# A decoder block's seven-product matrix multiplications: one product's halves set between the others, and one left factor split by itself a panel ahead

## The chip, the cores and the metric

The program runs on one core of one Trainium2 chip. The metric is the device time of one execution in microseconds (us). TensorE (PE in the profile) multiplies and writes PSUM; VectorE (DVE) and ScalarE (ACT) read PSUM and work on SBUF; GpSimd (POOL) takes part in a few elementwise steps and issues the DMAs that add to what is already in SBUF; SyncE (SP) issues the plain loads and stores. Each engine works through its own instructions in order and waits for the others by semaphores.

## What is computed

One layer of a decoder trunk on 512 tokens of width 1024, in float32: a norm and one wide projection; a retention branch and a dilated attention branch, each gated; an output projection; an MLP with a squared relu; a gated embedding. The parts that matter here:

```python
z  = rmsnorm(x, g_mix) @ w_in
y  = retention_chunkwise(rq, rk, rv)             # then group norm
ret_branch = (silu(rg) * y) @ w_ret_out
x  = x + (gate_r * ret_branch + gate_a * att_branch) @ w_o
u  = rmsnorm(x, g_mlp) @ w_up
x  = x + square(relu(u)) @ w_down
x  = x + sigmoid(rmsnorm(x, g_ple) @ w_ple_gate) * (p @ w_ple_proj)
```

## The kernel before

**Three products for one.** Every float32 product is made of three matmuls in a faster type. `split_unit` (L233 to L254) makes `whi` (ACT, L247, a rounding copy) and `wlo` (DVE, L248, the rest) out of a raw weight tile; `mm3` (L256 to L261) multiplies stationary high by moving high, stationary high by moving low, and stationary low by moving high. Activations are kept as such pairs too (`hh` and `hl`, `uh` and `ul`).

**Weights come by a plan.** `make_plan` lists all weight tiles (512 KB each, "units") in the order of use. `fetch` loads them into raw tiles (`wraw`, 6 buffers); `units(n)` hands out the next n and lets `ahead` split AHEAD more in advance (2 or 3) into `wsp` (4 buffers of `whi`, 4 of `wlo`). So a unit's split waits until the unit four before it has been multiplied.

**Seven products.** Five of the larger multiplications (the output projection `w_o` and the four slices of `w_down`) and two in the retention (its value and gate columns) are done block by block with seven products in place of eight. `SEVEN` (L35) is their order: a pair is product and half (u = 0, 1; which half of the 512-long contraction), and None means both halves at once. In `seven_products` (L1079) an entry with a half uses one unit: two column blocks p of the left factor, 2 k each, 3 matmuls, which makes 12 matmuls of 128x128 by 128x512. `BANK` (L36) says which PSUM bank a product is summed in: products 1, 6, 7, 4 share bank "b", products 5 and 3 share bank "c", product 2 has bank "a". There is one of each for p = 0 and 1. Banks b and c are of the pool `psg` (4 banks), bank a is of `psa` (4 banks), from which transposes and all the attention's and retention's small matmuls take theirs. When a product's second half is done, `after` reads the bank: in `w_o` and `w_down` by one DVE instruction that adds it, scaled, to the running rows `x` (L1112); in the retention by ACT copies (m5, m1, m3), and DVE adds. A product that goes into a shared bank waits for the reader of the product before it in that bank.

**Right factors.** Some of the seven right factors are plain blocks of the weight (B11 for product 1, B21 for 2, B22 for 3), the others sums of blocks: T1 (product 5), T2 (6), T3 (7), T4 (4). T2 is made by a DMA that adds a block into T1's raw tile after T1 is split (`chained`, L225, on POOL's queue); T3 in the same way from B22's tile, T4 from T2's. In the retention T1 and T4 are made by a DVE add of raw tiles instead (`added`, L220 to L223).

**Left factors.** A left operand lies in a tile `z` as eight slices of 256 columns for each of four row blocks j; slice 0 is the plain block of product 1, slice 1 that of product 2, and slices 3 to 6 are sums (`LEFT`, L39). `seven_left` (L1067) makes the sums by three DVE instructions (L1071, L1073) and then rounds and splits all seven slices in one pair of instructions, 1792 columns wide: `uh` on ACT (L1076), `ul` on DVE (L1077). Each has four tiles (j = 0 to 3) of the pool `bigp` (16 buffers).

**Where z comes from.** In the MLP (`tail`, L1153 on), a pass f runs four `cols_gemm` panels: jj = 0, 1 and, for each, b = 0 and 1. A panel makes two row blocks (n = 0, 1). `act` evacuates each by relu and square on ACT: with b = 0 slice 0 and a side tile `a21`, with b = 1 slices 1 and 2, after which it calls `seven_left`. So block j = 3 is finished by the last panel, and `seven_gemm` begins right behind it on PE. In `mix` (L1007), the same is done for `w_o` by the gated branches: slice 0 by L1037 at branch "r" with kk < 4, and the rest at kk >= 4 (L1042, L1045). `mix` and the first three MLP passes are put in order by the scheduler when the program is built, PE always; ACT and DVE are held in program order in the `w_o` product and in the last MLP pass.

**Work between the products.** `tick` is called once for each (product, p) and, on even counts (each count in the tail), lets waiting work in: in the retention's second seven products that is `ret_head` of the first two heads (L953 to L992: scores `rs`, states `kv`, values `ry`, transposes `pt`, each in a bank of `psa`); in the `w_o` product and the last `w_down` product transposes of finished rows (`gain_T`), four matmuls each.

Of the kernel before, what the change touches and what calls it, by code (L numbers as in the profile page):

```python
# [13 lines left out]
AF = mybir.ActivationFunctionType  # L14
ALU = mybir.AluOpType
# [16 lines left out]
WARM = 7  # L32
GG = (2, 4)

SEVEN = ((1, 0), (5, 0), (1, 1), (5, 1), (3, 0), (3, 1), (6, 0), (6, 1), (2, 0), (2, 1), (7, None), (4, None))  # L35
BANK = {1: "b", 2: "a", 3: "c", 4: "b", 5: "c", 6: "b", 7: "b"}  # L36
FACTOR = {1: "B11", 2: "B21", 3: "B22", 4: "T4", 5: "T1", 6: "T2", 7: "T3"}
SEVEN_UNITS = [(FACTOR[m], v) for m, u in SEVEN for v in ((0, 1) if u is None else (u,))]
LEFT = {1: 0, 2: 1, 4: 2, 7: 3, 5: 4, 6: 5, 3: 6}  # L39
# [37 lines left out]
def R(ap):  # L77
    return ap.bitcast(F32R)


class Block:
# [87 lines left out]
    def plan_seven(self, w, r0, c1, c2, vector=False):  # L169

        cols = (c1, c2)
        q = lambda i, j, u: w[r0 + 512 * i + 256 * u : r0 + 512 * i + 256 * (u + 1), cols[j] : cols[j] + 512]
        n = len(self.plan)
        at = lambda name, u: n + SEVEN_UNITS.index((name, u))
        for name, u in SEVEN_UNITS:
            if name == "T1":
                src = q(0, 1, u) if vector else (q(0, 1, u), q(0, 0, u))
                if vector:
                    self.added[at("B11", u)] = at("T1", u)
            elif name == "T4" and vector:  # L180
                self.added[at("B21", u)] = at("T4", u)
                src = (None, at("T2", u))
            elif name[0] == "B":
                src = q(int(name[1]) - 1, int(name[2]) - 1, u)
            else:
                prev, ij = {"T2": ("T1", (1, 1)), "T3": ("B22", (0, 1)), "T4": ("T2", (1, 0))}[name]
                k = at(prev, u)
                self.chained[k] = q(*ij, u)
                src = (None, k)
            self.plan.append((src, None))  # L190
# [23 lines left out]
    def ahead(self, n):  # L214
        while len(self.loaded) < min(len(self.plan), self.used + n):
            i = len(self.loaded)
            self.fetch(i + 1)
            raw, g0 = self.raws[i]
            self.loaded.append(self.split_unit(raw, g0))
            if i in self.added:  # L220
                self.fetch(self.added[i] + 1)
                total = self.raws[self.added[i]][0]
                self.nc.vector.tensor_tensor(total, total, raw, op=ALU.add)  # L223
            if i in self.chained:
                self.nc.gpsimd.dma_start(raw, self.chained[i].rearrange("(k p) n -> p k n", p=P), accum_op=ALU.add)  # L225

# [780 lines left out]
    def mix(self, A, O):  # L1007
        nc = self.nc
        U, Z = [[None] * 4, [None] * 4], {}
        for pair in ((0, 2), (1, 3)):  # L1010
            parts = {}
            for br, act, nk, bo in (("a", O, H, 24), ("r", A, KD, 16)):
                if pair[0] and br == "r":
                    self.load_x()
                for cc in pair:
                    sg = []

                    def gate(n, ps):
                        s = self.tmp("gs")
                        b = bo + 2 * cc + n  # L1020
                        nc.vector.tensor_tensor(s, ps, self.r_free, op=ALU.mult)
                        nc.scalar.activation(s, s, AF.Sigmoid, bias=self.gcol[:, b : b + 1])
                        sg.append(s)

                    def branch(n, ps):
                        t = self.tmp("gt")
                        nc.vector.tensor_tensor(t, sg[n], ps, op=ALU.mult)
                        kk = 2 * cc + n
                        if br == "a":
                            parts[kk] = t  # L1030
                            return
                        j = kk % 4
                        if kk < 4:
                            m = self.tmp("gm")
                            nc.gpsimd.tensor_tensor(m, t, parts[kk], op=ALU.add)
                            z = self.big("z").rearrange("p a (b t) -> p (a b) t", b=2)
                            nc.scalar.activation(z[:, 0], m[:, :256], AF.Copy)  # L1037
                            Z[j] = z, m[:, 256:]
                        else:
                            z, a21 = Z.pop(j)  # L1040
                            v = lambda ap: ap.rearrange("p (h t) -> p h t", h=2)
                            nc.vector.tensor_tensor(z[:, 1:3], v(t), v(parts[kk]), op=ALU.add)  # L1042
                            for part, n in zip(U, ("uh", "ul")):
                                part[j] = self.big(n)
                            self.seven_left(z, a21, U, j)  # L1045

                    self.cols_gemm(self.hT, KD, gate)
                    for h in range(H):
                        if br == "a":
                            self.force(("O", h, NG - 1))  # L1050
                            self.force(("split", h))
                        else:
                            for i in range(NT):
                                self.force(("A", h, i))
                    self.cols_gemm(act, nk, branch)
        return U

# [8 lines left out]

    def seven_left(self, z, a21, U, j):  # L1067

        nc = self.nc
        both = a21.unsqueeze(1).to_broadcast([P, 2, 256])  # L1070
        nc.vector.tensor_tensor(z[:, 3:5], z[:, 0:3:2], both, op=ALU.subtract)  # L1071
        for o, x, y in ((5, 4, 0), (6, 1, 5)):
            nc.vector.scalar_tensor_tensor(z[:, o], z[:, x], -1.0, z[:, y], op0=ALU.mult, op1=ALU.subtract)  # L1073
        w = lambda t: t.rearrange("p a b -> p (a b)")[:, : 7 * 256]
        hi, lo, src = w(U[0][j]), w(U[1][j]), z[:, 0:7].rearrange("p a b -> p (a b)")
        nc.scalar.activation(R(hi), src, AF.Copy)  # L1076
        nc.vector.tensor_tensor(R(lo), src, hi, op=ALU.subtract)  # L1077

    def seven_products(self, left, after):  # L1079

        banks, begun = {}, set()
        for m, half in SEVEN:
            us = self.units(2 if half is None else 1)
# [35 lines left out]
    def tail(self, mx):  # L1119
        nc, a = self.nc, self.a  # L1120
# [31 lines left out]

        h3 = None  # L1153
        for f in range(NF // 2):
            U = [[self.big("uh") for _ in range(4)], [self.big("ul") for _ in range(4)]]
            Z = {}

            def act(b, j, ps):
                r = self.tmp("ur")
                nc.scalar.activation(r, ps, AF.Relu)  # L1160
                if b == 0:
                    z = self.big("z").rearrange("p a (b t) -> p (a b) t", b=2)
                    a21 = self.tmp("a21")[:, :256]
                    Z[j] = z, a21
                    nc.scalar.activation(z[:, 0], r[:, :256], AF.Square)
                    nc.scalar.activation(a21, r[:, 256:], AF.Square)
                else:
                    z, a21 = Z[j]
                    nc.scalar.activation(z[:, 1:3], r.rearrange("p (h t) -> p h t", h=2), AF.Square)
                    self.seven_left(z, a21, U, j)  # L1170

            for jj in range(2):
                for b in range(2):
                    self.cols_gemm(h2, KD, lambda n, ps: act(b, 2 * jj + n, ps))
            ready = None
            if f == NF // 2 - 1:
                h3 = self.new_act(2, "h3")
                halves = [0] * NT

                def ready(t, j):  # L1180
                    self.gain_T(xs[t], t, j, h3, "h3", 3)
                    halves[t] += 1
                    if halves[t] == 2:
                        self.mean_squares(xs[t], 3, lambda mean: factor(t, mean))

                def factor(t, mean):
                    v = self.small(1, "v")
                    mean(v)
                    nc.gpsimd.tensor_tensor(r3[:, t : t + 1], v, self.mhalf[:, :1], op=ALU.pow)
            if f == NF // 2 - 1:  # L1190
                order = self.tc.manual_schedule(engines={nc.scalar.engine, nc.vector.engine})
                order.__enter__()
                self.AHEAD = 3
            self.seven_gemm(U, xs, f2, ready)
# [84 lines left out]
```

## Time and profile before

| | |
|---|---|
| median of 3 runs | 990.71 us (990.6 to 991.1) |
| the profiled execution | 991.26 us, of which the span of instructions is 989.4 us |
| granted clock of TensorE | 0.999 |
| the `w_o` product | about 551 to 600 us of the span |
| the four `w_down` products | begin at about 648, 731, 814 and 897 us |
| the retention's two seven products | about 290 to 382 us |

The profile page gives busy time by engine, forty slices of the span, the chain of work that ended last, the groups of instructions and the DMA issues. In its rows "A <- B" after a group names who ended the idle time of the engine just before it. In a timeline a row is: start, duration, engine, line, operation, tile written <- tiles read, shapes, count. A matmul's duration (about 0.39 us) is longer than the distance between two of them (about 0.23 us), because they overlap in the array; PE therefore counts as busy through short stalls.

### The profile page before, as it was taken

What the parts mean: (1) busy time and instruction counts of PE and PEld (TensorE: products, weight loads), DVE (VectorE), ACT (ScalarE), POOL (GpSimd) and SP (SyncE); (2) the same over time, 40 slices, a digit from 0 to 9 for tenths busy, and PEclk for the clock granted to TensorE, in tenths of its full rate; (3) what the DMA queues carried; (4) which work ended last, traced back from release to release, by engine and by line L of the source; (5) the groups of instructions that cost most, each with busy time, mean ns of one, the idle gap of its engine ahead of it and who ended that gap; (6) DMA issues with size and microseconds to landing.
All of it is one profiled execution on the core that took longest, in us unless ns stands there. A gap on an engine that the chain in (4) does not pass through costs nothing.

```text
span 989.4 us, 12438 instructions
## 1 busy us (share of the span) xinstructions
PE 979.3 (99%) x4540; PEld 816.5 (83%) x4540; DVE 646.9 (65%) x1009; ACT 491.0 (50%) x999; POOL 111.2 (11%) x108
## 2 busy tenths in 40 slices
PE   9999999999999999999999999999999999999998
PEld 6888899889888878888888788878887887887886
DVE  7857665775969878454643885577557467656753
ACT  6635344446646556342332467554654564465551
POOL 0310120220001220101002200020011002002000
PEclk9999999999999999999999999999999999999999
DMA  9822122334257734233544666567558548556811
GB/s 327 269 85 87 44 85 86 103 125 127 86 123 199 195 102 128 66 93 98 185 111 110 134 185 208 136 121 214 141 111 195 151 120 169 166 140 111 260 66 53
DMA packets 88508, 136.49 MB, mean 138 GB/s; under 512 B 6096, under 2 KB 40576, under 8 KB 88448
## 3 DMA queue, kind: packets, MB, share of 16 engines
q1 hardware_dynamic: 75248, 110.52, 34.6%
q0 software_dynamic: 13056, 25.17, 15.4%
q8 instruction: 35, 0.57, 0.2%
q14 instruction: 25, 0.20, 0.1%
q10 hardware_dynamic: 144, 0.02, 0.0%
HBM read 131.46 MB, written 4.24 MB: 137 GB/s over the span
## 4 chain that ended last, share of the span: by engine, by line
PE 90%; DVE 4%; issue 3%; ACT 2%; DMA 1%; POOL 0%; SPq 0%; ACTq 0%; DVEq 0%
PE pg L259 26%; PE pg L260 26%; PE pg L261 26%; DVE wlo L248 2%; ACT uh L1076 2%; PE po L724 1%; PE ph L577 1%; PE pa L261 1%; PE pa L259 1%; PE pa L260 1%; PE pt L335 1%; PE sc L701 1%; DVE x L1112 1%; PE pe L669 1%; DMA raw<-in_w_in 1%
## 5 line engine op out<-in xcount | busy, mean ns | idle before, releaser
L248 DVE TENSOR_TENSOR wlo<-raw,whi 128x1024 fp32r<-128x1024 f32 (+1 forms) x178 | 210.2, 1191 | 97.5 <-ACT whi L247 96.1
L247 ACT ACTIVATE whi<-raw 128x1024 fp32r<-128x1024 f32 (+1 forms) x177 | 182.0, 1034 | 183.4 <-PE pg L261 99.5
L259 PE MATMUL pg<-whi,hh 128*128 128x512 f32 x344 | 138.0, 402 | 0.0
L261 PE MATMUL pg<-whi,hl 128*128 128x512 f32 x344 | 134.7, 392 | 0.0
L260 PE MATMUL pg<-wlo,hh 128*128 128x512 f32 x344 | 134.5, 391 | 0.0
L259 PE MATMUL pg<-h2h,whi 128*128 128x512 f32 x256 | 99.6, 389 | 0.0
L260 PE MATMUL pg<-h2l,whi 128*128 128x512 f32 x256 | 99.6, 389 | 0.0
L261 PE MATMUL pg<-h2h,wlo 128*128 128x512 f32 x256 | 99.6, 389 | 0.0
L259 PE MATMUL pg<-whi,uh 128*128 128x512 f32 x240 | 96.0, 401 | 2.4 <-ACT whi L247 0.7
L260 PE MATMUL pg<-wlo,uh 128*128 128x512 f32 x240 | 93.6, 390 | 0.0
L253 DVE SCALAR_TENSOR_TENSOR wlo<-raw,gcol,whi 128x256 fp32r<-128x256 f32 (+1 forms) x144 | 66.2, 511 | 39.8 <-ACT whi L252 39.2
L261 PE MATMUL pg<-whi,ul 128*128 128x512 f32 x240 | 91.3, 390 | 0.0
L261 PEld LDWEIGHTS pg<-whi,hl 128*128 128x128 f32 x344 | 72.4, 210 | 11.1
L259 PEld LDWEIGHTS pg<-whi,hh 128*128 128x128 f32 x344 | 72.4, 211 | 10.9 <-DVE G L940 0.4
L252 ACT ACTIVATE whi<-raw,gcol 128x256 fp32r<-128x256 f32 (+1 forms) x144 | 65.7, 523 | 31.3 <-PE pg L261 15.5
L260 PEld LDWEIGHTS pg<-wlo,hh 128*128 128x128 f32 x344 | 72.6, 211 | 10.1
L259 PE MATMUL pg<-hh,whi 128*128 128x512 f32 x160 | 64.0, 400 | 0.0
L261 PE MATMUL pg<-hh,wlo 128*128 128x512 f32 x160 | 62.4, 390 | 0.0
L260 PE MATMUL pg<-hl,whi 128*128 128x512 f32 x160 | 62.3, 390 | 0.0
L259 PEld LDWEIGHTS pg<-whi,uh 128*128 128x128 f32 x240 | 45.0, 188 | 18.1 <-DVE x L1112 3.8
L259 PEld LDWEIGHTS pg<-h2h,whi 128*128 128x128 f32 x256 | 48.1, 188 | 10.0
L260 PEld LDWEIGHTS pg<-h2l,whi 128*128 128x128 f32 x256 | 48.1, 188 | 9.9
(222 smaller groups left out, 1751.1 us busy)
## 6 DMA issues: line engine op xcount, KB each, us to landing
raw<-in_w_in SPq DMA_DIRECT2D x72, 512.0 KB, 3.9
raw<-in_w_up SPq DMA_DIRECT2D x32, 512.0 KB, 4.5
raw<-in_w_down SPq DMA_DIRECT2D x32, 512.0 KB, 3.4
raw<-in_w_down POOLq DMA_DIRECT2D x32, 512.0 KB, 5.7
x<-in_x SPq DMA_DIRECT2D x8, 512.0 KB, 7.1
raw<-in_w_in POOLq DMA_DIRECT2D x8, 512.0 KB, 7.5
raw<-in_w_ret_out SPq DMA_DIRECT2D x8, 512.0 KB, 3.4
raw<-in_w_o SPq DMA_DIRECT2D x8, 512.0 KB, 3.3
```

The lines of the kernel that those rows point to most:

```text
L247: self.pin(nc.scalar.activation(R(hi[:, i]), raw[:, i], AF.Copy))
L248: nc.vector.tensor_tensor(R(lo[:, i]), raw[:, i], hi[:, i], op=ALU.subtract)
L252: self.pin(nc.scalar.activation(R(hi[:, i]), raw[:, i], AF.Copy, scale=g))
L253: nc.vector.scalar_tensor_tensor(R(lo[:, i]), raw[:, i], g, hi[:, i], op0=ALU.mult, op1=ALU.subtract)
L259: t.matmul(ps, sh, mh, start=first, stop=False, skip_group_check=more)
L260: t.matmul(ps, sh, ml, start=False, stop=False, skip_group_check=more)
L261: t.matmul(ps, sl, mh, start=False, stop=last, skip_group_check=more)
L335: nc.tensor.transpose(ps[:, k * P : (k + 1) * P], part[:, k * P : (k + 1) * P], self.ident)
L577: self.nc.tensor.transpose(ps[:, t * P : (t + 1) * P], rots[t][:, h * HD : (h + 1) * HD], self.ident)
L669: self.nc.tensor.transpose(ps[:, k * P : (k + 1) * P], e[:, k * P : (k + 1) * P], self.ident)
L701: nc.tensor.matmul(sc[:, h * P : (h + 1) * P], qT[:, h, rs], kT[:, h, rs], start=True, stop=True)
L1076: nc.scalar.activation(R(hi), src, AF.Copy)
```

## The change

Three edits. (1) In `SEVEN` the first half of product 2 moves ahead of product 3, and the second half stays behind product 6. Bank a of product 2 is therefore taken before product 3 and held until behind product 6. (2) Since B21's first half now comes ahead of T2 in the plan, the retention's DVE add that makes T4 out of T2 and B21 is hung on whichever of the two is split last. (3) `left_split` is a new function; slice 0 of a left factor is rounded and split by it alone (256 columns), as soon as slice 0 is there: in the MLP a panel ahead of the others (b = 0), in `mix` for both row blocks j of a panel at its first branch block (n = 0). `seven_left` splits the remaining six slices (1536 columns). The tiles `uh` and `ul` are allocated at the first of the two calls in place of ahead of the loop.

```diff
-SEVEN = ((1, 0), (5, 0), (1, 1), (5, 1), (3, 0), (3, 1), (6, 0), (6, 1), (2, 0), (2, 1), (7, None), (4, None))
+SEVEN = ((1, 0), (5, 0), (1, 1), (5, 1), (2, 0), (3, 0), (3, 1), (6, 0), (6, 1), (2, 1), (7, None), (4, None))
...
-                    self.added[at("B11", u)] = at("T1", u)
+                    self.added[at("B11", u)] = at("T1", u), at("B11", u)
             elif name == "T4" and vector:
-                self.added[at("B21", u)] = at("T4", u)
+                self.added[max(at("B21", u), at("T2", u))] = at("T2", u), at("B21", u)
...
-                self.fetch(self.added[i] + 1)
-                total = self.raws[self.added[i]][0]
-                self.nc.vector.tensor_tensor(total, total, raw, op=ALU.add)
+                self.fetch(max(self.added[i]) + 1)
+                total, part = (self.raws[k][0] for k in self.added[i])
+                self.nc.vector.tensor_tensor(total, total, part, op=ALU.add)
...
+                            if n == 0:
+                                for i in (j, j + 1):
+                                    self.left_split(Z[i][0], U, i, 0, 1)
                             z, a21 = Z.pop(j)
...
-                            for part, n in zip(U, ("uh", "ul")):
-                                part[j] = self.big(n)
...
-        w = lambda t: t.rearrange("p a b -> p (a b)")[:, : 7 * 256]
-        hi, lo, src = w(U[0][j]), w(U[1][j]), z[:, 0:7].rearrange("p a b -> p (a b)")
-        nc.scalar.activation(R(hi), src, AF.Copy)
-        nc.vector.tensor_tensor(R(lo), src, hi, op=ALU.subtract)
+        self.left_split(z, U, j, 1, 7)
+
+    def left_split(self, z, U, j, a, b):
+
+        if U[0][j] is None:
+            for part, n in zip(U, ("uh", "ul")):
+                part[j] = self.big(n)
+        hi, lo = (part[j].rearrange("p a b -> p (a b)")[:, 256 * a : 256 * b] for part in U)
+        src = z[:, a:b].rearrange("p a b -> p (a b)")
+        self.nc.scalar.activation(R(hi), src, AF.Copy)
+        self.nc.vector.tensor_tensor(R(lo), src, hi, op=ALU.subtract)
...
-            U = [[self.big("uh") for _ in range(4)], [self.big("ul") for _ in range(4)]]
+            U = [[None] * 4, [None] * 4]
...
                     nc.scalar.activation(a21, r[:, 256:], AF.Square)
+                    self.left_split(z, U, j, 0, 1)
```

## The prediction

> **What bounds the kernel now.** I read the page's first part, then the waits of the weight loads, then the timeline of PE at the head of a down product.
>
> ```profile
> span 989.4 us, 12438 instructions
> PE 979.3 (99%) x4540; PEld 816.5 (83%) x4540; DVE 646.9 (65%) x1009; ACT 491.0 (50%) x999; POOL 111.2 (11%) x108
> 604.00:640.00 36.00, 36.00 (x160) 29.83 (x159) 20.05 (x38) 24.54 (x50) 2.42 (x3) 1.00 0.64 176
> ```
>
> PE is the bound everywhere: 979.3 of 989.4 us. The third row is a stretch of an up projection in the windows view (PE first, then weight loads, DVE, ACT, POOL, clock): 159 weight loads in 36.00 us make 0.2267 us from matmul to matmul. Since one matmul lasts 0.39, a stall under 0.16 us never shows as idle, so I count stalls by starts. The change takes no matmul away; it can win only stalls. The waits view gives them for the weight loads (total, times, longest):
>
> ```profile
> PEld pg L259 <- DVE x L1112: 3.8, 9, 0.5
> PEld pg L259 <- ACT whi L247: 3.2, 6, 1.2
> PEld pg L259 <- ACT uh L1076: 2.9, 5, 0.9
> PEld pt L335 <- DVE At L990: 2.0, 2, 1.4
> PEld pg L261 <- DVE ul L1077: 0.4, 1, 0.4
> ```
>
> All but the fourth row belong mainly to the heads of the seven-product stages: 9 and 5 times are two and one in each of four down products, and one in the output projection. PE in the first down product:
>
> ```profile
> 655.24 0.39 PE L260 MATMUL pg<-wlo,uh 128*128 128x512 f32 x1
> 655.71 0.50 PE L259 MATMUL pg<-whi,uh 128*128 128x512 f32 x1
> ...
> 659.26 0.39 PE L261 MATMUL pg<-whi,ul 128*128 128x512 f32 x1
> 659.67 1.06 PE L259 MATMUL pg<-whi,uh 128*128 128x512 f32 x2
> ...
> 660.88 0.50 PE L259 MATMUL pg<-whi,uh 128*128 128x512 f32 x1 [0.15 <-DVE x L1112]
> 661.22 0.39 PE L260 MATMUL pg<-wlo,uh 128*128 128x512 f32 x1
> ```
>
> From 655.24 to 661.22 there are 20 steps, which at 0.2267 would take 4.53 us; they take 5.98. **1.44 us** are lost, in two places: 0.35 at 655.71, where PE wants `uh` of block j = 3, and the rest from 659.67 on, where it wants a split weight and then bank after bank that DVE has not yet read. The four down products are alike: the same stretch of the first and of the last, in the windows view, holds the same number of instructions on every engine:
>
> ```profile
> 655.25:661.20 5.95, 5.64 (x21) 3.53 (x20) 5.52 (x6) 3.46 (x4) 1.20 (x1) 1.00 0.81 139
> ...
> 904.45:910.40 5.95, 5.65 (x21) 3.54 (x20) 5.52 (x6) 3.46 (x4) 1.20 (x1) 1.00 0.78 139
> ```
>
> That makes 4 x 1.44 = **5.76 us**. The output projection:
>
> ```profile
> 557.59 0.39 PE L261 MATMUL pg<-whi,ul 128*128 128x512 f32 x1
> 558.46 0.50 PE L259 MATMUL pg<-whi,uh 128*128 128x512 f32 x1 [0.48 <-ACT uh L1076]
> ...
> 560.52 1.20 PE L261 MATMUL pg<-whi,ul 128*128 128x512 f32 x4
> 562.45 1.23 PE L259 MATMUL pg<-whi,uh 128*128 128x512 f32 x3 [0.73 <-ACT whi L247]
> 563.52 0.40 PE L260 MATMUL pg<-wlo,uh 128*128 128x512 f32 x1
> ```
>
> 16 steps (3.63 us) take 5.93: **2.30 us** lost. In all 8.06 us stand at these five heads.
>
> **The change, part by part.** *Slice 0 split early.* A down product starts on PE at 648.0 and now needs, in order: (1,0) and (5,0) of j = 0, 1 (24 matmuls), (1,1) of j = 2, 3 (12), then (5,1). Before, (1,1) with k = 3 wanted block 3's whole split; now it wants slice 0 alone, which is ready a panel (24 x 2 x 0.2267 = 10.9 us) earlier. The first to want the late split is (5,1) with k = 3, after 36 matmuls and, with the k = 2 ones of both p first, 42: 648.0 + 42 x 0.2267 = 657.5. The late split on DVE and its neighbours, whole:
>
> ```profile
> 653.43 0.42 DVE L1073 SCALAR_TENSOR_TENSOR z<-z 128x256 f32<-128x256 f32 x1
> 655.68 2.03 DVE L1077 TENSOR_TENSOR ul<-z,uh 128x1792 fp32r<-128x1792 f32 x1 [1.83 <-ACT uh L1076]
> 657.62 1.22 DVE L248 TENSOR_TENSOR wlo<-raw,whi 128x1024 fp32r<-128x1024 f32 x1
> 658.76 2.72 DVE L1112 SCALAR_TENSOR_TENSOR x<-pg,f,x 128x512 f32<-128x512 f32 x4
> ```
> ```profile
> 651.14 1.06 ACT L247 ACTIVATE whi<-raw 128x1024 fp32r<-128x1024 f32 x1 [0.73 <-PE pg L261]
> 653.95 1.70 ACT L1076 ACTIVATE uh<-z 128x1792 fp32r<-128x1792 f32 x1 [1.75 <-DVE z L1073]
> ```
>
> From 1.06 for 1024 and 1.70 for 1792 columns, ACT takes 0.83 ns a column and 0.21 us fixed; DVE, from 1.22 and 2.03, 1.05 ns and 0.14. So 1536 columns take 1.49 and 1.76: `uh` ends at 655.4 and `ul` at 657.2, ahead of 657.5 (its first reader comes two matmuls later still). The stall of 0.35 goes; margin 0.3 to 0.7 us. The price: 20 more instructions of 256 columns on ACT (0.21 + 0.21 = 0.42 each) and on DVE (0.14 + 0.27 = 0.41), laid into the panel:
>
> ```profile
> 665.00:725.00 60.00, 60.00 (x267) 49.69 (x266) 36.69 (x58) 31.30 (x58) 4.10 (x4) 1.00 0.64 167
> ```
>
> There ACT is busy 31.30 and DVE 36.69 of 60 us while PE has no gap: cost nothing. Behind the new ACT instruction queue only weight splits of units used a panel later; without that cover each would cost its 0.42. The tiles `uh` and `ul` are asked for a panel earlier than they were written, 5.4 us after the product before has read them: no wait.
> [...]
>
> *Product 2's half.* (2,0) puts 12 matmuls = 2.72 us between (5,1) and (3,0), on a bank of its own. (5,1) now ends at about 658.9, (2,0) at 661.6. The four x reads (2.72 us; two of product 1, two of 5) started at 658.76, because DVE was late; product 1 now ends about 656.4 and product 5 at 658.9. Behind `ul` at 657.2 and one weight split (1.22) the four end at 661.1, and (3,0) with p = 0 needs only the third. The 1.09 us behind 659.26 go. What is late next: DVE, which still has ul, two splits and four reads in 655.4 to 662.4. (2,0)'s own weight takes the place in the split order of product 3's first (ACT 651.14), so it is ready by 653.5. Bank b: product 7 now has 12 matmuls instead of 24 behind product 6's reads; one read is 0.68, cover 2.72.
>
> *Queues.* B21's load moves ahead of B22's two on SP, all from 6 tiles that come free as before or sooner. T1's adding DMA and T2 to T4's keep their order on POOL; T3 and T4 have five units (13.6 us) in place of six from split to split:
>
> ```profile
> L225 POOL DMA_DIRECT2D raw<-in_w_down x24: 1203/1203/1224, 640.0 to 913.5; - x24
> DMA to landing us min/median/max: 5.5/6.2/9.7
> ```
>
> 1.2 to issue and 9.7 at worst to land: covered. In the retention the moved DVE add is 1.22 us as before, and B21's raw tile is held three units longer, five of six; the sixth serves the loads.
>
> *The retention pays.* Bank a there is two of the four `psa` banks; it was held for 24 matmuls (5.4 us) and now for 72 (16.3). The heads' values are slow to leave theirs:
>
> ```profile
> 343.41 0.59 PE L986 MATMUL ry<-st,qT 128*128 128x256 f32 x2
> 347.45 0.59 PE L984 MATMUL ry<-v,rsT 128*128 128x256 f32 x2
> 351.05 1.05 PE L964 MATMUL rs<-qT,hT 128*128 128x128 f32 x8
> 351.94 0.60 PE L972 MATMUL kv<-v,kd 128*128 128x256 f32 x2
> ```
> ```profile
> 347.99 0.48 DVE L990 SCALAR_TENSOR_TENSOR At<-ry,r,G 128x256 f32<-128x256 f32 x1 [0.46 <-POOL r L325]
> 351.31 0.48 DVE L990 SCALAR_TENSOR_TENSOR At<-ry,r,G 128x256 f32<-128x256 f32 x1 [0.44 <-POOL r L325]
> 352.57 0.48 DVE L990 SCALAR_TENSOR_TENSOR At<-ry,r,G 128x256 f32<-128x256 f32 x1 [0.66 <-POOL r L325]
> 368.91 0.44 PE L335 MATMUL pt<-ident,At 128*128 128x128 f32 x2 [1.01 <-DVE At L990]
> ```
>
> One is held from 343.4 to 348.5, 5.1 us. With two banks only, `rs` (now at 351.05) waits for 351.8 and `kv` (351.94) for 353.05: about 1.1 us. The second head's values, in the same hold, can do the same again: upper bound 2.2 us, if the builder leaves PE's order; lower bound -1.2, the stall of 1.01 idle (1.18 by starts) at 368.9, which product 2's banks make already and another order may lose. I take +0.6.
>
> **Sum.** Against the profiled execution: 991.26 - 8.06 + 0.6 = 983.8. It lies 0.55 above the median 990.71; from the median, **983.3 us**.
>
> **The rivals.** *A, DVE becomes the bound at the heads.*
>
> ```profile
> 648.00:661.50 13.50, 11.48 (x13) 1.00 0.61 119
> ```
>
> DVE is busy 11.48 of 13.50 there. If the builder sets two x reads (1.5 us) ahead of `ul`, that ends at 658.7, some 0.9 late: up to 4 x 0.9 = 3.6 returned, 986.9. Against it: 0.54 us of DVE work leaves this stretch. [...]
> *B, the order doesn't come about:* PE's order is the builder's, and before it put two matmuls of T2 ahead of product 3. If (2,0) gains nothing, only the `uh` waits go: 4 x 0.35 + 0.97 (558.46 and 560.52) = 2.4, 988.3.
> *C, slower: the banks.* If no side work of the heads can be put off, each of the five pairs during bank a's hold waits 5.1 - 2.72 = 2.4 us: 11.9 in all, 991 - 8.1 + 11.9 = 994.5. It beats the gain from 1.6 us a pair on. Against it: the waits view has two waits for At before, and the builder may set the side work later. [...]
>
> **Chances.** Forecast 0.75 (981.5 to 985.5), A 0.13, B 0.07, C 0.05. Range 981.5 to 988.0. A measurement tells 0.2% (2 us): faster means under 988.7. Faster 0.87, the same 0.08, slower 0.05.
>
> **What would show it.** Right: no step over 0.3 us on PE in the first 60 matmuls of each of the five heads; `uh` in 1536 and 256 columns at about 1.49 and 0.42; the x reads of product 1 ended before (2,0) ends; the weight load waits on x L1112, uh and ul near nothing. Wrong: PE waiting for `x` or `ul` there (A), a T2 weight ahead of product 3 again (B), PE waiting for At, rs or kv between 335 and 382 us (C).

## The result, and the profile after

| | median us | runs | ratio to before, 95% interval |
|---|---|---|---|
| before | 990.9 (990.6 to 991.45) | 4 | |
| changed | 983.41 (983.28 to 983.9) | 4 | 0.9925 [0.9908, 0.9942] |

The kernel became faster by 0.75%, and the measured median lies 0.11 us above the forecast of 983.3. The profiled execution took 983.3 us against 991.26. First the page of the changed kernel: span, busy time by engine, and the chain that ended last.

```profile
span 981.2 us, 12477 instructions
PE 973.4 (99%) x4540; PEld 817.3 (83%) x4540; DVE 649.7 (66%) x1029; ACT 492.5 (50%) x1019; POOL 110.8 (11%) x108
PE 97%; DVE 1%; POOL 1%; ACT 0%; DMA 0%; issue 0%; SPq 0%; ACTq 0%
```

and the same chain in the kernel before, where VectorE and ScalarE still had a part:

```profile
PE 90%; DVE 4%; issue 3%; ACT 2%; DMA 1%; POOL 0%; SPq 0%; ACTq 0%; DVEq 0%
```

TensorE has the same 4540 matmuls and is busy for 5.9 us less: at the heads the record of a matmul that had to wait is longer (0.50 us in place of 0.39 at 655.71 in the kernel before), and only 2.3 of the 8.2 us by which the span fell were idle time of TensorE. DVE and ACT have the 20 new instructions each (1009 to 1029, 999 to 1019). So the time came out of stalls, as it had to. The waits of the weight loads in the changed kernel:

```profile
PEld rs L964 <- DVE At L990: 1.3, 1, 1.3
PEld pt L335 <- DVE At L990: 1.0, 2, 0.7
PEld ry L984 <- DVE At L990: 0.5, 1, 0.5
...
PEld kv L972 <- DVE At L990: 0.3, 1, 0.3
PEld pg L259 <- ACT whi L247: 0.3, 1, 0.3
PEld pg L261 <- DVE ul L1085: 0.2, 1, 0.2
```

The waits for `x` (3.8 us, 9 times) and `uh` (2.9, 5 times) are gone, and that for `whi` fell from 3.2 to 0.3. Three waits for `At` of the retention (`rs`, `ry`, `kv`, 2.1 us together) are new, and those of `pt` fell from 2.0 to 1.0. The windows view of the first 13.5 us of the first down product, changed kernel and then the kernel before (columns: stretch, length, then busy time and count of PE, weight loads, DVE, ACT, POOL; clock, DMA share, GB/s):

```profile
645.80:659.30 13.50, 13.50 (x61) 11.20 (x60) 12.95 (x14) 7.79 (x8) 3.61 (x3) 1.00 0.63 138
```
```profile
648.00:661.50 13.50, 13.20 (x55) 9.77 (x54) 11.48 (x13) 8.14 (x9) 3.61 (x3) 1.00 0.61 119
```

Six more matmuls in the same time; 6 x 0.2267 = 1.36 us for each head. Counted by starts (each step over 0.26 us, less 0.227), the lost time by stretch, in the two profiled executions:

| us lost | before | changed | difference |
|---|---|---|---|
| first 20 us (loads, first products) | 2.94 | 2.16 | -0.78 |
| retention, second seven products (334 to 383) | 3.75 | 4.43 | +0.68 |
| output projection's stage (548 to 602) | 2.99 | 0.77 | -2.22 |
| heads of the four down products | 4 x 1.39 | 0 | -5.56 |
| all other stretches | 6.93 | 6.93 | 0 |
| whole span | 22.17 | 14.29 | -7.88 |

The spans differ by 8.2 us, so the table holds nearly all of it. (A part of what remains stands behind small matmuls. Their own steps are mostly 0.11 or 0.22 us, but the step from the first 512-column matmul behind them to the next is 0.31 to 0.44 us at 80 places of the changed kernel, which make 9.5 of its 14.29 us: 2.3 of the 4.43, 0.70 of the 0.77, 6.5 of the 6.93, none in the first 20 us. The kernel before has 78, 9.2 us.)

### The profile page after: what moved, and what is told of

Read it like the earlier page. It is cut to its first block, busy times and chain, and to the rows that moved or that the text cites. A ratio compares the mean times of both kernels' runs of the same rounds, so it can differ in the third digit from the quotient of the medians.

```text
span 981.2 us, 12477 instructions
## 1 busy us (share of the span) xinstructions
PE 973.4 (99%) x4540; PEld 817.3 (83%) x4540; DVE 649.7 (66%) x1029; ACT 492.5 (50%) x1019; POOL 110.8 (11%) x108
## 4 chain that ended last, share of the span: by engine, by line
PE 97%; DVE 1%; POOL 1%; ACT 0%; DMA 0%; issue 0%; SPq 0%; ACTq 0%
PE pg L259 29%; PE pg L261 29%; PE pg L260 29%; PE po L724 1%; PE ph L577 1%; PE pa L261 1%; PE pa L259 1%; PE pa L260 1%; PE pt L335 1%; PE sc L701 1%; PE pe L669 1%; PE kv L972 1%; PE sc L707 1%; PE ry L984 1%; POOL r L325 0%; DVE wlo L248 0%
## 5 line engine op out<-in xcount | busy, mean ns | idle before, releaser
L261 PE MATMUL pg<-whi,ul 128*128 128x512 f32 x240 | 93.4, 390 | 0.0
L1085 DVE TENSOR_TENSOR ul<-z,uh 128x256 fp32r<-128x256 f32 (+1 forms) x40 | 43.2, 1090 | 28.3 <-ACT uh L1084 27.7
L261 PEld LDWEIGHTS pg<-h2h,wlo 128*128 128x128 f32 x256 | 48.0, 188 | 10.0
```

The costliest lines, as they stand in the source:

```text
L261: t.matmul(ps, sl, mh, start=False, stop=last, skip_group_check=more)
L1085: self.nc.vector.tensor_tensor(R(lo), src, hi, op=ALU.subtract)
```

## The experiments

Eleven kernels were run. Each was timed beside the kernel before (medians of 990.8 to 991.0 us); the last column is the lost time by starts at the four heads and in the output projection's stage, from the profiled run. "Changed" below means the kernel of the change.

| kernel | median us | ratio, 95% interval | heads / output projection |
|---|---|---|---|
| before | 990.9 | | 5.56 / 2.99 |
| changed | 983.41 | 0.9925 [0.9908, 0.9942] | 0 / 0.77 |
| e1: product 2's place only | 985.28 | 0.9944 [0.9931, 0.9956] | 1.34 / 0.99 |
| e2: early split only | 983.9 | 0.993 [0.9917, 0.9944] | 0.28 / 1.21 |
| e3: changed, old order in both retention stages | 982.76 | 0.9921 [0.9909, 0.9934] | 0 / 0.78 |
| e4: changed, product 2 first in both retention stages | 983.34 | 0.9928 [0.9915, 0.994] | 0 / 0.78 |
| e5: changed, bank a held longer in the retention | 986.16 | 0.9955 [0.9941, 0.9969] | 0 / 0.77 |
| e6: changed, retention with old order, then product 2 first | 981.79 | 0.9909 [0.9896, 0.9923] | 0 / 0.78 |
| e7: changed, late split in six pieces | 984.29 | 0.9935 [0.9922, 0.9949] | 0 / 0.71 |
| e8: as e6, with the old order outside the retention | 982.17 | 0.9916 [0.9903, 0.993] | 0.29 / 1.21 |
| e9: as e2, late split padded to the old width | 988.17 | 0.9973 [0.9963, 0.9983] | 4.21 / 1.60 |
| e10: kernel before, one DVE instruction held back | 986.33 | 0.9952 [0.994, 0.9964] | 1.36 / 2.56 |
| e11: as e9, the same instruction held back | 985.99 | 0.9955 [0.9943, 0.9968] | 1.68 / 1.77 |

### Which edit frees the heads: e1 and e2

The theory was the prediction's: two waits of their own, `uh` (0.35 us a head) which only the early split removes, and `x` with the weight behind it (1.09) which only product 2's new place removes. The rival: both come from one late chain.

e1 keeps the new `SEVEN` and takes the early split back out (one split of 1792 columns):

```diff
-        self.left_split(z, U, j, 1, 7)
+        w = lambda t: t.rearrange("p a b -> p (a b)")[:, : 7 * 256]
+        hi, lo, src = w(U[0][j]), w(U[1][j]), z[:, 0:7].rearrange("p a b -> p (a b)")
...
```

> The order of the products is the changed one; the left factor is split as before, all seven slices at once behind the last panel. My theory: the two waits at a head are separate. The bank and split waits (1.09 us in each down product, about 1.33 in the output projection) go, the wait for uh stays (0.35 in each down product, 0.97 in the output projection), the retention costs its +0.6: 990.9 - 5.7 + 0.7 = about 985.9 us. Rival 1: the order does nearly all and the half of product 2 covers the late split too: 983.5. Rival 2: the split was what mattered, since a late split delays everything behind it: over 988.

e2 keeps the early split and takes `SEVEN` back:

```diff
-SEVEN = ((1, 0), (5, 0), (1, 1), (5, 1), (2, 0), (3, 0), (3, 1), (6, 0), (6, 1), (2, 1), (7, None), (4, None))
+SEVEN = ((1, 0), (5, 0), (1, 1), (5, 1), (3, 0), (3, 1), (6, 0), (6, 1), (2, 0), (2, 1), (7, None), (4, None))
```

> Slice 0 is split by itself a panel ahead; the order of the products is that of before. My theory: the wait for uh goes (4 x 0.35 + 0.97 = 2.4 us), the waits for x and for a split weight at the start of product 3 stay, the retention is as before: about 988.5 us. Rival 1 (the order does nearly all): 990.5. Rival 2 (the split does nearly all): 984.

e1 came as expected (985.28): what is left is the wait for `uh`, in e1's waits view:

```profile
PEld pg L259 <- ACT uh L1076: 2.4, 5, 0.5
```

e2 did not: 983.9 in place of 988.5. With the old order of the products, the early split removes 5.28 of the 5.56 us at the heads, the waits for `x` among them, which it was said not to touch. e1 saves 5.6 us, e2 7.0, both together 7.5: the edits cover the same loss. The DVE timeline of the changed kernel shows why:

```profile
648.31 0.68 DVE L1072 TENSOR_TENSOR z<-z,a 128x512 f32<-128x512 f32 x1
649.03 0.89 DVE L1074 SCALAR_TENSOR_TENSOR z<-z 128x256 f32<-128x256 f32 x2
649.83 1.22 DVE L248 TENSOR_TENSOR wlo<-raw,whi 128x1024 fp32r<-128x1024 f32 x1
651.53 1.76 DVE L1085 TENSOR_TENSOR ul<-z,uh 128x1536 fp32r<-128x1536 f32 x1 [0.48 <-ACT uh L1084]
653.20 0.75 DVE L1120 SCALAR_TENSOR_TENSOR x<-pg,f,x 128x512 f32<-128x512 f32 x1
```

and that of the kernel before:

```profile
651.24 0.68 DVE L1071 TENSOR_TENSOR z<-z,a 128x512 f32<-128x512 f32 x1
651.96 0.42 DVE L1073 SCALAR_TENSOR_TENSOR z<-z 128x256 f32<-128x256 f32 x1
652.30 1.22 DVE L248 TENSOR_TENSOR wlo<-raw,whi 128x1024 fp32r<-128x1024 f32 x1
```

Before, a weight split of 1.22 us stood between the last two slice sums of block 3; after, the two sums run together and the weight split follows while ACT makes `uh`. So `ul` ended 9.49 us behind the head's first matmul before (648.22), and 7.52 behind it after (645.77): 1.97 us earlier, of which the smaller size of `uh` and `ul` can give 0.21 + 0.27 for block 3, and as much again for block 2, whose split stands ahead of it in the same chain. The first read of `x` moved from 10.54 to 7.43, and the third from 11.86 to 9.89, which is 1.97 as well (the weight split that stood ahead of the first read now stands behind it). e1's trace has the order of before (first `x` at 10.54), e2's that of after (7.43). This gave a new theory: DVE's order at this place, which the builder chooses, makes the loss; the rival to it is the late split's length.

### Length or order: e9, e10, e11

e9 gives e2's late split its old width back, with an eighth slice that no product reads (the extra ACT copy in the panel fills it):

```diff
...
+                    nc.scalar.activation(z[:, 7], r[:, :256], AF.Square)
...
-        self.left_split(z, U, j, 1, 7)
+        self.left_split(z, U, j, 1, 8)
```

> As e2 (slice 0 split early, order of products as before), but the late split is 1792 columns wide again: it also does an eighth slice that nothing uses (a second copy of slice 0, made in the panel before by one more ACT instruction). Theory: what frees the head is the dependence, that product 1 no longer waits for the late split, so that its reads on DVE come ahead of product 3's need: 984 to 985 us. Rival: it is the shorter late split (0.21 us on ACT, 0.27 on DVE for a block): back to about 987 or more, with the waits of product 3 for x.

988.17: the number of the rival, and the heads lose 4.21 us again. But its DVE timeline had changed in its order as well as in the length, so that it settled nothing by itself:

```profile
649.43 0.68 DVE L1073 TENSOR_TENSOR z<-z,a 128x512 f32<-128x512 f32 x1
650.15 0.43 DVE L1075 SCALAR_TENSOR_TENSOR z<-z 128x256 f32<-128x256 f32 x1
650.50 1.22 DVE L248 TENSOR_TENSOR wlo<-raw,whi 128x1024 fp32r<-128x1024 f32 x1
651.63 0.42 DVE L1075 SCALAR_TENSOR_TENSOR z<-z 128x256 f32<-128x256 f32 x1
653.41 0.75 DVE L1121 SCALAR_TENSOR_TENSOR x<-pg,f,x 128x512 f32<-128x512 f32 x1 [1.36 <-PE pg L261]
654.08 2.02 DVE L1086 TENSOR_TENSOR ul<-z,uh 128x1792 fp32r<-128x1792 f32 x1
```

The weight split stands between the sums again, and a read of `x` stands ahead of `ul`. e10 and e11 therefore ask for one thing alone: the third weight split that the program has behind a block's sums must be issued after the second of these sums. e10 does it in the kernel before, which keeps every other instruction; e11 does it in e9.

```diff
+    sums = [None] * 9
...
-                nc.vector.tensor_tensor(R(lo[:, i]), raw[:, i], hi[:, i], op=ALU.subtract)
+                self.sums.append(None)
+                with self.tc.issue_after(self.sums[0].ins) if len(self.sums) == 4 else nullcontext():
+                    nc.vector.tensor_tensor(R(lo[:, i]), raw[:, i], hi[:, i], op=ALU.subtract)
...
-            nc.vector.scalar_tensor_tensor(z[:, o], z[:, x], -1.0, z[:, y], op0=ALU.mult, op1=ALU.subtract)
+            self.sums = [nc.vector.scalar_tensor_tensor(z[:, o], z[:, x], -1.0, z[:, y], op0=ALU.mult, op1=ALU.subtract)]
```

> The kernel before, with all its instructions as they are (one split of seven slices, 1792 columns, the old order of the products); one VectorE weight split per seven-product multiplication is held behind the last two slice sums of block 3, where it stood between them. Theory, that this place in VectorE's order costs the heads and neither the split apart nor the order of the products is needed: the last split of the slices ends at about 8.0 us behind the head's first matmul (9.50 in the kernel before, 7.52 in the changed one), product 1's rows are read from about 7.9 us on, and each down head loses 0.1 to 0.5 us in place of 1.39: 985.0 to 987.4 us, likeliest 986. Rival, that slice 0's own early split is what frees the head: the heads go on losing over 1 us each, 989.5 to 991. Second rival, that the held weight split is then missed on TensorE: 988 to 990 with a wait on wlo at the heads.

> The kernel with the early split of slice 0 and a late split padded to the old width (an unused eighth slice), which took 988.17 us and lost 0.93 to 1.40 us at each down head, now with the same VectorE weight split held behind the last two slice sums. By the theory of VectorE's order the heads lose 0.1 to 0.3 us each and the time is 983.9 to 985.0 us, near the 983.9 us of the early split with the short late one. Rival, that the late split's length itself is what was lost (0.48 us of it on each head and its readers behind it): 986.5 to 988.2 us.

e10's timeline at the same place, and its weight-load waits:

```profile
651.37 0.89 DVE L1077 SCALAR_TENSOR_TENSOR z<-z 128x256 f32<-128x256 f32 x2
652.18 1.22 DVE L252 TENSOR_TENSOR wlo<-raw,whi 128x1024 fp32r<-128x1024 f32 x1
654.09 2.03 DVE L1081 TENSOR_TENSOR ul<-z,uh 128x1792 fp32r<-128x1792 f32 x1 [0.69 <-ACT uh L1080]
656.03 1.22 DVE L252 TENSOR_TENSOR wlo<-raw,whi 128x1024 fp32r<-128x1024 f32 x1
657.16 2.72 DVE L1116 SCALAR_TENSOR_TENSOR x<-pg,f,x 128x512 f32<-128x512 f32 x4
```
```profile
PEld pg L263 <- ACT uh L1080: 2.0, 5, 0.5
...
PEld pg L263 <- DVE x L1116: 1.5, 5, 0.4
```

986.33, as expected: holding one DVE instruction back in each multiplication, with no instruction added or shortened, saves 4.6 us, against the change's 7.5. (`ul` ended 8.48 us behind the head's first matmul, later than the 8.0 expected.) DVE's order in e10 differs from that of before in these five instructions alone, and ACT's not at all; but the builder also gave a few of TensorE's matmuls at the four down heads other places. All reads of `x` come 1.01 us earlier behind the head's first matmul (the first at 9.53 in place of 10.54), and each head loses 0.34 in place of 1.39. For e11 neither side was wholly right. The median falls by 2.2 us from e9's (988.17 to 985.99), where besides the order of the sums the read of `x` ahead of `ul` is gone too; the heads lose 0.42 each, more than the 0.1 to 0.3 expected; the time lies above the range for the order (985.0) and below the rival's (986.5). So the length counts as well: from e11 to e2, which differ in the late split's width, in e9's extra ACT copy and in where the builder puts the weight splits among the reads of `x`, the median falls by 2.1 us and the heads by 1.40.

The traces of the five kernels with the old order of the products show what joins order and length. Times in this table are us behind the head's first matmul; the third read of `x` is the one for which, by the prediction's reckoning, product 3 waits.

| down heads of | `ul` ends | first read of `x` starts | third read starts | lost at one head |
|---|---|---|---|---|
| before | 9.49 | 10.54 | 11.86 | 1.39 |
| e9, the first three | 9.68 | 7.00 | 11.39 | 0.94 |
| e9, the fourth | 9.49 | 10.54 | 11.86 | 1.41 |
| e11, the first three | 8.48 | 8.40 | 10.85 | 0.42 |
| e11, the fourth | 8.47 | 9.52 | 10.84 | 0.42 |
| e10 | 8.48 | 9.53 | 10.85 | 0.34 |
| e2, the first three | 7.51 | 7.43 | 9.89 | 0.07 to 0.11 |
| e2, the fourth | 7.52 | 8.57 | 9.89 | 0 |

The loss goes with the third read, not with the first; e10, where TensorE's order is another, agrees with e11 to 0.08 us. In the rows of e9 and then of e11 the two reads of a row are the third and the fourth, of about 0.74 us each: the third ends at 658.55 in e9 and at 658.14 in e11, and TensorE goes on 0.06 us later.

```profile
657.81 1.40 DVE L1121 SCALAR_TENSOR_TENSOR x<-pg,f,x 128x512 f32<-128x512 f32 x2
658.61 0.50 PE L259 MATMUL pg<-whi,uh 128*128 128x512 f32 x1 [0.55 <-DVE x L1121]
```
```profile
657.40 1.40 DVE L1125 SCALAR_TENSOR_TENSOR x<-pg,f,x 128x512 f32<-128x512 f32 x2
658.20 0.50 PE L263 MATMUL pg<-whi,uh 128*128 128x512 f32 x1 [0.15 <-DVE x L1125]
```

Of the 1.97 us by which the change brings this read forward, the order of the sums gives 1.01 (11.86 to 10.85, e10) and the length 0.96 (10.85 to 9.89, e11 to e2). The 0.96 is twice 0.21 + 0.27, for blocks 2 and 3: the weight split behind block 2's `ul` starts 1.88 us behind the head's first matmul in e11 and 1.40 in e2.

In one line, heads and output projection added, each step on top of those before it: 8.55 us lost before; the order of the sums takes 4.63 (e10); the early slice 0.47 (e11: 0.79 less in the output projection, 0.32 more at the heads); the shorter late split 1.96 (e2); product 2's place, last, 0.72 (changed). Taken first, product 2's place covers 6.22 of the same 8.55 (e1), and the early slice without a shorter late split 2.74 (e9).

### The pieces' fixed cost: e7

The late split is made in six instructions a block in place of one: 100 more on ACT and 100 more on DVE.

```diff
-        self.left_split(z, U, j, 1, 7)
+        for s in range(1, 7):
+            self.left_split(z, U, j, s, s + 1)
```

> The changed kernel with the six late slices split one by one: 100 more ACT and 100 more DVE instructions of 256 columns (0.42 and 0.41 us each, of which 0.21 and 0.14 are the fixed part). Theory (the late split has about 2 us of margin at each head in the changed kernel, and pieces on DVE follow those on ACT one by one): no loss over 0.5 us: 983.4 to 983.9. Rival (the fixed part stands on the path of the five heads, 5 x 0.21 on ACT for the last block): 983.4 + 5 x 1.05 = 988.7.

984.29, which is 0.4 above the expected range and 0.9 above the changed kernel with overlapping intervals, and no stall at any head. The first 13.5 us of its first down product (from 648.05, for e7):

```profile
648.05:661.55 13.50, 13.50 (x61) 11.21 (x60) 12.54 (x20) 8.35 (x13) 3.61 (x3) 1.00 0.73 159
```

The same 61 matmuls as in the changed kernel, with 20 DVE instructions in place of 14. Its profiled run lost 4.49 us in the first 20 us of the span, 2.33 more than the changed kernel's, before the first piece is made (456.5); that is more than the whole difference of the spans (983.4 and 981.2). Behind the first 20 us the two profiled runs lost the same, 12.09 us in e7 and 12.13 in the changed kernel.

### What the retention pays: e3, e4, e5, e6, e8

All of these give the retention's stages (pr = 0 and 1) their own orders and leave the five other stages as changed, but for e8. e3 puts the old order there:

```diff
+SEVEN_R = ((1, 0), (5, 0), (1, 1), (5, 1), (3, 0), (3, 1), (6, 0), (6, 1), (2, 0), (2, 1), (7, None), (4, None))
...
-            self.seven_products(left, after)
+            self.seven_products(left, after, SEVEN_R)
...
```

> The changed kernel with the order of before in the retention's two seven-product stages alone. My theory: the retention's waits of scores and values for At (0.9 us and more) come from product 2's banks being held for 72 matmuls; they go, and the wait of the transposes for At at 24 matmuls' hold comes back as before (about 1.2 by starts): 983.4 - 0.7 = 982.7 us. Rival: the difference of the retention between the two traces is chance or lies in the loads: 983.4.

982.76, as expected: the retention gives back 0.65 us by the medians (the intervals overlap), 0.70 by the stalls (4.43 to 3.73). The changed kernel's PE timeline at the place that the prediction named:

```profile
350.18 0.39 PE L259 MATMUL pg<-whi,us 128*128 128x512 f32 x1
351.49 1.16 PE L964 MATMUL rs<-qT,hT 128*128 128x128 f32 x8 [0.92 <-DVE At L990]
352.75 0.70 PE L972 MATMUL kv<-v,kd 128*128 128x256 f32 x2
```

`rs` waits for a bank of `psa` until DVE has read the values before it. e4 starts both stages with product 2, so that its banks are given back before the heads' work comes; e5 takes them right behind (1, 0) and holds them for 108 matmuls in place of 72. The first line is e4's, the second e5's; in e4 ACT also copies out product 2's bank in place of product 1's, and product 1's reader adds:

```diff
+SEVEN_R = ((2, 0), (2, 1), (1, 0), (5, 0), (1, 1), (5, 1), (3, 0), (3, 1), (6, 0), (6, 1), (7, None), (4, None))
+SEVEN_R = ((1, 0), (2, 0), (5, 0), (1, 1), (5, 1), (3, 0), (3, 1), (6, 0), (6, 1), (2, 1), (7, None), (4, None))
```

> The changed kernel with product 2 ahead of all others in the retention alone (its bank is copied out by ACT, and product 1's reader adds), so that its two banks are held for 24 matmuls while only scores and states use the pool. My theory: no wait for At is left there (about 1.8 us by starts in the changed kernel); against it, product 7 now follows product 6 at once in one bank, up to 0.7 us each in two stages: 981.6 to 983. Rival: banks don't matter there: 983.4 or more.

> The changed kernel, but in the retention product 2's first half goes in right behind product 1's first half, so that its two banks are held for 108 matmuls in place of 72. My theory (held banks are what the heads' side work waits for): more and longer waits of scores and values for At in the second stage, 1 to 4 us more than the changed kernel by starts: 984.5 to 987.5 us. Rival (a wait for At is a chance of the build order, whatever the hold): within 0.4 us of 983.4.

e4 took 983.34, above the range of the theory (981.6 to 983) and at its rival's number, but not for the rival's reason: the second stage lost only 1.93 us and no wait for `At` was left, but the first stage lost 2.42 in place of 0.28: the weight splits there wait 9.8 us for loads, 2.3 in the changed kernel. e5 slowed down by 2.75 us, within its range, but not for its reason: the second stage lost 4.17, no more than the changed kernel, and the first 2.81. That a longer hold costs more waits for `At` is not shown. The waits of weight loads on TensorE that the first stage added, in e4 and in e5, and the wait of ACT's weight splits for loads, in e4 and in the changed kernel (290 to 334 us of the span):

```profile
PEld pg L262 <- ACT whi L250: 1.9, 1, 1.9
```
```profile
PEld pg L263 <- DVE wlo L251: 2.1, 1, 2.1
```
```profile
ACT whi L250 <- DMA raw<-in_w_in: 9.8, 3, 4.6
```
```profile
ACT whi L247 <- DMA raw<-in_w_in: 2.3, 1, 2.3
```

So e6 takes the old order for the first stage, and product 2 first, with the banks read as in e4, for the second:

```diff
+SEVEN_R = (((1, 0), (5, 0), (1, 1), (5, 1), (3, 0), (3, 1), (6, 0), (6, 1), (2, 0), (2, 1), (7, None), (4, None)),
+           ((2, 0), (2, 1), (1, 0), (5, 0), (1, 1), (5, 1), (3, 0), (3, 1), (6, 0), (6, 1), (7, None), (4, None)))
...
-            self.seven_products(left, after)
+            self.seven_products(left, after, SEVEN_R[pr])
...
```

> The changed kernel with the order of before in the retention's first stage and product 2 ahead of all in its second stage alone, where the heads' side work runs. Theory: no wait for At (2.0 us of weight-load waits in the kernel with the old order there), and none of the load waits that the first stage had with product 2 first: 982.8 - 1.8 = 981.0 us. Rival: the second stage too gets load waits or a wait between products 6 and 7: 982 to 983.5.

**981.79 us is the best time**: 9.1 below the kernel before and 1.6 below the changed one, though 0.8 above the 981.0 expected. In its waits view no wait for `At` is left, and the second stage lost 1.89 us (3.75 before). The PE timeline of e6 where `rs` waited:

```profile
350.77 0.39 PE L265 MATMUL pg<-whi,hl 128*128 128x512 f32 x1
351.00 1.05 PE L968 MATMUL rs<-qT,hT 128*128 128x128 f32 x8
351.88 0.60 PE L976 MATMUL kv<-v,kd 128*128 128x256 f32 x2
```

e8 asks what product 2's place is worth at the heads once the early split is there: e6 with the old `SEVEN` in the output projection and the down products.

> As e6, but with the order of before in the output projection and the down products, so that of the change only the early split is left there. Theory after e2 (the early split alone frees the heads): 0.3 to 0.8 us over e6, so 981.3 to 981.8. Rival (moving product 2's half still brings what it brought without the split, about 5 us): 986.

982.17, which is 0.4 above the 981.3 to 981.8 expected and 0.38 above e6 with overlapping intervals; the stalls are larger by 0.72 in those five stages (0.29 and 1.21 against 0 and 0.78). By these profiled runs it is worth 0.7 us there; the medians alone do not show a difference.

## Why the prediction was right, and where its steps were not

**The total.** 8.06 us of stalls at five heads less 0.6: measured, 7.78 went (5.56 and 2.22) and 0.68 came in the retention, 7.1 net. The profiled run fell by 8.0 because its first 20 us lost 0.78 less; nothing was changed there. The medians fell by 7.5. So part of the closeness is luck: 0.8 of the profiled run's 8.0 us came from a stretch that the change does not touch. The heads were counted a little high: 1.44 us each in the prediction, 1.39 by the steps over 0.26.

**"The stall of 0.35 goes; margin 0.3 to 0.7 us."** The stall went. The margin was mis-sized: `ul` was to end at 657.2, 9.2 us behind 648.0, and ended 7.52 behind the first matmul. The sum kept `uh`'s start where it was (653.95) and only shortened the two instructions. That block 2's split ahead of it is shorter too was not carried into it, although rival A counts both (0.54 us of DVE work less). That the weight split at 652.30, between two sums in the timeline, could change its place was not asked, although the prediction itself said that the order is the builder's. The place gave 1.01 us of the 1.97, the two lengths 0.96.

**"The 1.09 us behind 659.26 go" by product 2's half.** True of the edit by itself: e1 leaves 0.33 of 1.39 a head, all of it the wait for `uh`. But the step that failed is the splitting of the loss into two waits with one remedy each, which made rival B's price: "If (2,0) gains nothing, only the `uh` waits go", 988.3. e2 is that case, and it took 983.9. Everything behind the late sums (`uh`, `ul`, the reads of `x`) moves with them, so the early split brings the third read forward, and product 2's half covers its lateness: the two remedies meet the same loss. Where the late split stays as long and the sums stay apart (e9, 988.17), the early split comes out near that price.

**The pieces cost nothing.** Right: `uh` took 1.491 us for 1536 columns and 0.399 for 256 in the rows of after, against 1.49 and 0.42 worked out; `ul` 1.76 and 0.41. e7, with 200 more, has no stall at the heads. The pieces do take time: in e7 ACT is busy for 503.7 us against 492.5 in the changed kernel, DVE for 653.9 against 649.7. The heads without a stall show that this time is not on the path.

**The retention, +0.6.** Measured +0.68, at the named place: `rs` started at 351.05 before and starts at 351.49 in a run that was 0.8 us ahead after its first 20 us, so it is 1.2 late where 1.1 was worked out. `kv` behind it waits 0.3 and `ry` 0.5, and the longest wait of `pt` fell by half, from 1.4 to 0.7, which pays part of it back. The lower bound, that another order may lose the wait which product 2's banks already make, was real and not even the lowest: e6's second stage loses 1.9 us less than before.

**The rivals.** A: DVE was full, as it said (12.95 of 13.50 us), but the reads of `x` did not delay `ul`, and nothing was lost. In e9 one read does stand ahead of `ul`. C: the banks cost 0.7 us, not 11.9. (Its sum as written gives 994.8; the 994.5 comes from 990.71 less 8.06.)

**Not settled.** Why the builder places the weight split differently for the shorter late split: its own reckoning is in no trace. e9 has an ACT copy more in the panel besides the width, so which of the two turns the order there is open too.

## What to carry to other kernels

When several waits follow each other at one place, ask first whether they hang on one late chain; then the remedies cover the same loss and their prices do not add. Where a builder orders an engine, look in the timeline for what stands inside the late chain (here 1.22 us of work that nobody waited for yet, between two short sums): holding that one instruction back gave 4.6 of 7.5 us. Then ask which single read the next product waits for: here the loss followed the third of four, wherever the first one stood. And give each stage the order that its own banks and loads want: the same list of products was right in five stages, and cost 0.7 us in a sixth that wanted product 2 first.

## What the runs showed of the hardware that was not expected

- The first 20 us differ from run to run of nearly the same work: between 1.77 us (e3) and 4.49 (e7) of lost time by starts in the profiled runs, though the first 1436 matmuls of TensorE are the same, in the same order, in all the kernels here. Single profiles that differ by less than the 2.7 us between these two are therefore read here by stretch, not by span.
- A full engine cost nothing here. From 652.80 to 658.80 DVE has no idle time in the changed kernel (6.00 of 6.00 us), and TensorE has no stall (no step from matmul to matmul is over 0.227 us; windows view, columns as above):

```profile
652.80:658.80 6.00, 6.00 (x28) 4.99 (x27) 6.00 (x8) 2.13 (x2) 2.11 (x2) 1.00 0.69 152
```
